# Last chunk of the FFN's second product: T1 and T2 unsplit in DRAM, loads in order of use, last pair's sums on GpSimd, T3 multiplied behind B22

## The chip, the cores and the metric

The kernel runs on one core of one Trainium2 chip. The metric is the device time of one execution in microseconds (us), lower is better. A core has TensorE (PE in the profile; its weight loads are PEld), VectorE (DVE), ScalarE (ACT) and GpSimd (POOL), each with a queue of its own that is worked off in order, and SyncE (SP), whose queue issues this kernel's DMA transfers, also in order.

## The reference

Two layers on a sequence of 1024 positions with 1024 channels. Each layer is a token mixer (FoX attention in layer 0, gated linear attention in layer 1) and then a SwiGLU channel mixer. Only the channel mixer matters here:

```python
def swiglu(h, w_in, w_out):
    gate, up = jnp.split(h @ w_in, 2, axis=-1)
    return (jax.nn.silu(gate) * up) @ w_out
...
        h = modulate(rms_norm(x, norm2_g[i]), sh2, sc2)
        x = x + g2[:, None, :] * swiglu(h, ffn_w_in[i], ffn_w_out[i])
    return rms_norm(x, final_g)
```

The hidden width is 2816, that is 22 tiles of 128 channels. `h @ w_in` is called the first product below, `(...) @ w_out` the second product.

## The kernel before, in words

Channels lie on the 128 partitions, positions along the free dimension, in two halves of 512. Every fp32 operand is split into a rounded high part (`hi`, made by an ACT copy) and the remainder (`lo`, a subtraction, mostly on DVE); a block product is then three matmuls, hi by hi, hi by lo and lo by hi (`mm3`, L304 to L307). Both products are computed by a Strassen-like scheme on 2 by 2 blocks with seven block products instead of eight. Its right-hand operands have the names B11, T1, T2, T3, B21, T4, B22: the B are quarters of the hidden activations, the T are sums and differences of them. A block product over four pairs of hidden tiles is 4 x 3 = 12 matmuls of 128x128 by 128x512.

The first product leaves the hidden activations in DRAM (`hid_out`, L1582). B11, B21, B22, T1 and T2 are written already split, as 512 KB tiles of hi and lo; T3 and T4 (`RAWT`) are written unsplit, 256 KB each, and are split when they come back.

The second product runs over the 11 pairs of hidden tiles in three chunks of 3, 4 and 4 pairs (`ODS`). Chunks 0 and 1 loop over four pairs of output tiles (i = 0 to 3), with seven block products each, in PSUM tiles that the profile names `p`; their results are added up by DVE in SBUF (L1860). In the last of these passes the five sums per output pair that undo the scheme (L1874 to L1878), and the four gate-and-residual steps (L1880), follow each pair; the sums are on GpSimd for i = 0 to 2 and on VectorE for i = 3. The residual is loaded by `load_xr` into four small buffers, the cycle `late_raw`, which unsplit T3 and T4 also use.

The last chunk (L1909 to L1940) multiplies for each group g = 0 to 3 of output tiles B11, T1, T2, B22 and T3, in PSUM tiles `f0a`, `f0b` (layer 0) and `f1a`, `f1b` (layer 1); `pa` takes B11, T2 and T3 one after another, and DVE adds its state to the output (`out_add`, L1899) between them. Then B21 and T4 follow over all output tiles (`f0e`, `f1e`), with the sums of squares for the next norm.

`part(c_)` (L1759) is a generator that loads the 28 tiles of a chunk, one per step, and splits the unsplit ones; `advance(n)` drives it to step n at written places between the products. For the last chunk the order is B11, T1, T2, B22, T3, B21, T4, four tiles each. Unsplit tiles are loaded up to three steps ahead. A tile can only be loaded when the block product of the chunk before that read its slot is done.

Weights are loaded raw (`op_raw`, L920, tiles `xv`), four of them per group, combined by three or four GpSimd operations (L938, L939, L940 and L950 or L956) and split (L174 on ACT, L175 on DVE; tiles `o`). They run about five block products ahead, as far as their six slots reach.

The program's text gives priorities. The order on each engine is fixed before the run by a scheduler that works from its own estimate of the times, so a product can stand on the engine earlier or later than in the text, unless a dependency forbids it. `tc.issue_after(x)` adds such a dependency on order alone.

Of the kernel before, what the change touches and what calls it, by code (L numbers as in the profile page):

```python
# [9 lines left out]
F32 = mybir.dt.float32  # L10
# [6 lines left out]
P = 128  # L17
S = 1024
# [35 lines left out]
def trunk(ctx, tc, x, c, ada_w, ada_b, norm1_g, norm2_g, ffn_w_in, ffn_w_out,  # L54
          fox_w_in, fox_b_f, fox_w_out, gla_w_in, gla_w_a2, gla_b_a, gla_g_o,
          gla_w_out, final_g, out, dbg=None, stop=None):
    nc = tc.nc
# [281 lines left out]
    xr = Ring(big, take(8))  # L339
# [62 lines left out]
    for t in range(6):  # L402
        nt, src = (4, rows2[0:8, :]) if t < 4 else (2, crow)
# [20 lines left out]
    def mcol(l, j, k):  # L424
        return modc[:, l, j, k:k + 1]
# [10 lines left out]
    def last_of(e):  # L436
        return next(i for i in reversed(nc.cur_bb.bb.instructions) if i.engine == ENG[e])
# [753 lines left out]
    for n, (d, hf) in enumerate(rest0):  # L1191
# [25 lines left out]
        if n in late_tr:  # L1217
            tp, i = late_tr[n]
# [258 lines left out]
    early = [s_ for s_ in rest if s_ in list(vring.q) + qk_all + list(cumr.q)]  # L1477
# [14 lines left out]
    def ffn(l, oh, xs, slots, nm, mid, norm_end, each=None, blocks=None):  # L1492
# [19 lines left out]
        hi = lambda t: t[:, 0]  # L1512
        lo = lambda t: t[:, 1]
# [59 lines left out]
        hid_d = {}  # L1573
        for i in range(NPR):
            for nm_ in ("B11", "B12", "B21", "B22", "T1", "T2", "T3", "T4"):
                if nm_ == "B12":
                    continue
                raw_ = nm_ in RAWT
                hid_d[(nm_, i)] = tc.dram_tile([P, HALF] if raw_ else [P, 2, HALF], F32,
                                               name=f"hid{l}_{nm_}{i}")  # L1580

        def hid_out(nm_, i, y):  # L1582

            if nm_ not in RAWT:
# [75 lines left out]
        B11, B21 = b["B11"], b["B21"]  # L1660
# [43 lines left out]
        B12, B22, T1, T2 = b["B12"], b["B22"], b["T1"], b["T2"]  # L1704
# [26 lines left out]
        T3 = b["T3"]  # L1731
# [4 lines left out]
        T4 = b["T4"]  # L1736
# [22 lines left out]
        def part(c_):  # L1759

            raw_ = late_raw if c_ else early_raw
            n_k = ODS[c_]
            nms = ONAMES if c_ < OC - 1 else ENAMES
            order = list(range(7 * n_k)) if c_ else list(FIRST)
            tiles, ys = o[c_], {}
            for nm_ in ONAMES:
                tiles[nm_] = [None] * n_k
            at = lambda n: (nms[n // n_k], n % n_k)

            def load_raw(n):  # L1770
                nm_, k = at(n)
                if nm_ in RAWT and n not in ys:
                    ys[n] = raw_()
                    nc.sync.dma_start(ys[n], hid_d[(nm_, OAT[c_] + k)])

            for j, n in enumerate(order):
                nm_, k = at(n)
                t = tiles[nm_][k] = big.tile([P, 2, HALF], FR, tag=SL[c_][n], name=f"{nm_}o{l}{c_}{k}")
                load_raw(n)
                if nm_ in RAWT:  # L1780
                    split_t(t, ys[n])
                else:
                    nc.sync.dma_start(t.bitcast(F32), hid_d[(nm_, OAT[c_] + k)])
                for ahead in order[j + 1:j + 4]:
                    load_raw(ahead)
                yield

        xr, zs = {}, {}

        def load_xr(i, views):  # L1790
            for a in range(2):
# [42 lines left out]
        for c_ in range(OC - 1):  # L1834
            last = c_ == OC - 2
            spare = (9, 2)[c_]
            n_nxt[0] = 0
            nxt[0] = part(c_ + 1)
            for i in range(4):
                Y1, Y3 = (xs[2 * i][:, hsl(hf)] for hf in range(2))  # L1840
                Y2, Y4 = (xs[2 * i + 1][:, hsl(hf)] for hf in range(2))
                Z1, Z5 = zs[i][:, 0], zs[i][:, 1]

                def p_(j):
                    ps = prod(feed.next(), o[c_][ONAMES[j]])
                    if i < 3:
                        advance(spare * (7 * i + j + 1) // 21)
                    else:
                        advance(UPTO[c_][j])
                    if last and j == (2 if i < 3 else 4):  # L1850
                        if i == 3:
                            sv.extend(Views(sb[0:2], 2, [HALF], f"se{l}").v)
                        load_xr(i, late_raw if i < 3 else Cycle(sv))
                    return ps

                def onto(y, ps, first=True):
                    if c_ == 0 and first:
                        nc.scalar.copy(y, ps)
                    else:
                        nc.vector.tensor_add(y, y, ps)  # L1860
# [12 lines left out]
                V = nc.vector if i == 3 else nc.gpsimd  # L1873
                V.tensor_add(Y1, Y1, Z1)  # L1874
                V.tensor_add(Y4, Y4, Z1)
                V.tensor_sub(Y2, Y4, Y2)
                V.tensor_add(Y4, Y4, Z5)
                V.tensor_sub(Y3, Y4, Y3)  # L1878
                for (a, hf), v_ in (((0, 0), Y1), ((1, 0), Y2), ((1, 1), Y4), ((0, 1), Y3)):
# [9 lines left out]
        def chained(ps, nm_, start, behind=(), cs=slice(0, HALF)):  # L1889
            w, t = feed.next(), oe[nm_]  # L1890
            for k in range(4):
                with ExitStack() as es:
                    for ins in behind if k == 0 else ():
                        es.enter_context(tc.issue_after(ins))
                    mm3(ps, w.hi[:, k, :], w.lo[:, k, :], hi(t[k])[:, cs], lo(t[k])[:, cs],
                        start and k == 0, k == 3, True)

        def out_add(m, hf, ps):
            nc.vector.scalar_tensor_tensor(xs[m][:, hsl(hf)], ps, mcol(l, 5, m), xs[m][:, hsl(hf)],  # L1899
                                           op0=ALU.mult, op1=ALU.add)  # L1900
# [5 lines left out]

        tmp = None if each else Views(slots["to"], 2, [HALF], f"te{l}")
        sq = SumFew(sv, 0)
        for g in range(4):  # L1909
            if g == 3:  # L1910
                feed.depth = 3
            pa, pb = (pj([P, HALF], F32, f"f{l}{nm_}{g}") for nm_ in "ab")
            chained(pa, "B11", True)
            advance(20 + (8 * (5 * g + 1)) // 15)
            out_add(2 * g, 1, pa)
            chained(pb, "T1", True)
            advance(20 + (8 * (5 * g + 2)) // 15)
            out_add(2 * g + 1, 0, pb)
            chained(pa, "T2", False)
            advance(20 + (8 * (5 * g + 3)) // 15)  # L1920
            out_add(2 * g, 0, pa)
            chained(pb, "B22", False)
            advance(20 + (8 * (5 * g + 4)) // 15)
# [55 lines left out]
    order = ex_sl + slots["hid"] + slots["b"][4:] + slots["to"] + x_slots + slots["b"][:4]  # L1979
# [540 lines left out]
```

## Time and profile before

| | us |
|---|---|
| runs of the kernel, three | 2356.21, 2358.49, 2358.67 |
| their median | 2358.49 |
| the profiled execution's own time | 2358.25 |
| its span, first to last instruction | 2356.5 |
| DVE, ACT and POOL busy in the span | 1778.1, 1122.5, 1126.3 |

A row of the timeline gives the start, the duration, the engine, the line, the operation with output and inputs, and in brackets the idle time of the engine in front of it and what ended it. A row of the windows view gives, for a stretch of the span, each engine's busy time (with the number of its instructions), the TensorE clock that was granted (1.00 is full), the busy share of the DMA engines and the rate. DMA rows under `SPq` give the issue, not the transfer. Matmuls overlap, so the pace is read from start to start.

### The profile page before, as it was taken

How to read it: one execution, taken by the hardware profiler on the slowest of the kernel's cores; microseconds unless marked ns; L12 is line 12 of the kernel's file. 1: busy time of each engine (PE TensorE's matmuls, PEld its weight loads, DVE VectorE, ACT ScalarE, POOL GpSimd, SP SyncE). 2: the span in 40 equal slices, each digit the busy share in tenths (PEclk: the TensorE clock that was granted, in tenths of full speed). 3: DMA queues.
4: the chain of work that ended last, by engine and by line, in shares of the span. 5: the costliest groups of instructions: out<-in, count | busy, mean ns of one | idle time of the engine just before them, and what ended most of it. 6: DMA issues, size and time to landing. Idle time of an engine off the chain costs nothing. (4 is left out here: it accounts for less than half of the span.)

```text
span 2356.5 us, 35548 instructions
## 1 busy us (share of the span) xinstructions
PE 2327.9 (99%) x12168; PEld 1980.9 (84%) x12168; DVE 1778.1 (75%) x2957; ACT 1122.5 (48%) x2166; POOL 1126.3 (48%) x995
## 2 busy tenths in 40 slices
PE   8999999999999999999999999999999999999999
PEld 7888888888888888888878898898888888888878
DVE  6578787886788888886787665678787777876776
ACT  6656655665443333345234644344453333345235
POOL 1334544533445666664643431345446665665631
PEclk8999999999999999999999999999999999999999
DMA  8423333332435545458674442554435444458574
GB/s 266 144 90 106 102 121 95 121 129 96 143 101 167 187 161 173 160 192 298 224 272 158 138 134 87 146 182 166 145 111 164 165 150 155 148 204 298 199 277 136
DMA packets 349614, 383.38 MB, mean 163 GB/s; under 512 B 25372, under 2 KB 286648, under 8 KB 349432
## 3 DMA queue, kind: packets, MB, share of 16 engines
q1 hardware_dynamic: 349432, 381.11, 49.1%
q8 instruction: 96, 1.57, 0.3%
q14 instruction: 86, 0.70, 0.1%
HBM read 279.76 MB, written 101.25 MB: 162 GB/s over the span
## 5 line engine op out<-in xcount | busy, mean ns | idle before, releaser
L174 ACT CAST o_s<-xv_s 128x512 fp32r<-128x512 f32 (+1 forms) x392 | 236.5, 610 | 343.0 <-PE p_b L307 250.0
L175 DVE TENSOR_TENSOR o_s<-xv_s,o_s 128x512 fp32r<-128x512 f32 (+1 forms) x392 | 331.9, 851 | 44.8 <-ACT o_s L174 44.0
L307 PE MATMUL p_b<-B,o_s 128*128 128x512 f32 x608 | 236.0, 389 | 0.0
L306 PE MATMUL p_b<-B,o_s 128*128 128x512 f32 x608 | 235.9, 389 | 0.0
L305 PE MATMUL p_b<-B,o_s 128*128 128x512 f32 x608 | 235.4, 390 | 0.0
L938 POOL TENSOR_TENSOR ex_s<-xv_s,xv_s 128x512 f32<-128x512 f32 (+1 forms) x64 | 96.2, 1503 | 259.0 <-DMA xv_s<-in_ffn_w_in_dram 119.9
L1291 POOL TENSOR_SCALAR lp_s<-lp_s,st 128x128 f32<-128x128 f32 (+7 forms) x128 | 98.0, 769 | 246.3 <-DVE st L1290 231.1
L305 PE MATMUL p_b<-T,o_s 128*128 128x512 f32 x480 | 186.8, 389 | 0.0
L306 PE MATMUL p_b<-T,o_s 128*128 128x512 f32 x480 | 186.7, 389 | 0.0
L307 PE MATMUL p_b<-T,o_s 128*128 128x512 f32 x480 | 181.1, 389 | 0.0
L307 PEld LDWEIGHTS p_b<-B,o_s 128*128 128x128 f32 x608 | 114.1, 188 | 23.8
L305 PEld LDWEIGHTS p_b<-B,o_s 128*128 128x128 f32 x608 | 114.2, 188 | 23.7 <-DVE x L1657 0.2
L306 PEld LDWEIGHTS p_b<-B,o_s 128*128 128x128 f32 x608 | 114.2, 188 | 23.5
L1289 ACT ACTIVATE lp_s<-lp_s,st 128x128 f32<-128x128 f32 (+7 forms) x128 | 99.3, 776 | 58.0 <-DVE st L1285 56.7
L940 POOL TENSOR_TENSOR xv_s<-ex_s,xv_s 128x512 f32<-128x512 f32 (+1 forms) x64 | 94.4, 1475 | 59.5 <-DVE o_s L175 56.5
L1657 DVE TENSOR_TENSOR ex_s<-ex_s,p_b 128x512 f32<-128x512 f32 x140 | 94.3, 682 | 37.4 <-PE p_b L307 37.3
L174 ACT CAST pt_s<-t_b 128x512 fp32r<-128x512 f32 (+1 forms) x160 | 79.7, 547 | 72.9 <-PE t_b L1311 72.3
L950 POOL TENSOR_TENSOR xv_s<-xv_s,xv_s 128x512 f32<-128x512 f32 x48 | 65.2, 1358 | 96.3 <-issue 52.3
L175 DVE TENSOR_TENSOR pt_s<-t_b,pt_s 128x512 fp32r<-128x512 f32 (+1 forms) x160 | 96.3, 630 | 15.9 <-ACT pt_s L174 15.4
L246 POOL TENSOR_TENSOR w_l_s<-w__s,w_h_s 128x256 fp32r<-128x256 f32 x90 | 69.4, 799 | 76.6 <-ACT w_h_s L242 58.8
L307 PEld LDWEIGHTS p_b<-T,o_s 128*128 128x128 f32 x480 | 90.1, 188 | 18.7
L306 PEld LDWEIGHTS p_b<-T,o_s 128*128 128x128 f32 x480 | 90.1, 188 | 18.6
(1532 smaller groups left out, 7396.8 us busy)
## 6 DMA issues: line engine op xcount, KB each, us to landing
xv_s<-in_ffn_w_in_dram SPq DMA_DIRECT2D x176, 256.0 KB, 3.2
hid_B<-x SPq DMA_DIRECT2D x66, 512.0 KB, 2.8
ad_s<-in_ada_w_dram SPq DMA_DIRECT2D x384, 64.0 KB, 2.3
hid_T<-x SPq DMA_DIRECT2D x44, 512.0 KB, 2.9
xv_s<-in_ffn_w_out_dram SPq DMA_DIRECT2D x88, 256.0 KB, 3.2
ada_s<-in_ada_w_dram SPq DMA_DIRECT2D x96, 128.0 KB, 2.8
T2o<-hid_T SPq DMA_DIRECT2D x22, 512.0 KB, 7.6
T1o<-hid_T SPq DMA_DIRECT2D x22, 512.0 KB, 8.6
```

The source lines that it names most:

```text
L174: nc.scalar.copy(hi, src)
L175: nc.vector.tensor_sub(lo, src, hi.bitcast(F32))
L246: (nc.gpsimd if i < 3 else nc.vector).tensor_sub(lo[:, cs], rw[:, cs], hi[:, cs].bitcast(F32))
L305: nc.tensor.matmul(ps, ah, bh, start=start, stop=False, skip_group_check=chain)
L306: nc.tensor.matmul(ps, ah, bl, start=False, stop=False, skip_group_check=chain)
L307: nc.tensor.matmul(ps, al, bh, start=False, stop=stop, skip_group_check=chain)
L938: nc.gpsimd.tensor_add(s1, a21, a22)
L940: nc.gpsimd.tensor_sub(a11, s1, a11)
L950: nc.gpsimd.tensor_sub(r[A12], r[A12], r[A11])
L1289: nc.scalar.activation(lp, lp, AF.Exp, bias=mcur, scale=-1.0, accum_out=st[:, qi, 2:3])
L1291: nc.gpsimd.tensor_scalar(lp, lp, st[:, qi, 3:4], 1.0, op0=ALU.mult, op1=ALU.mult)
L1657: nc.vector.tensor_add(d, d if src is None else dest(G, src), ps)
```

## The change

For the last chunk's four pairs (i from 7 to 10) T1 and T2 are also written unsplit. When they come back, ACT makes hi and GpSimd makes lo. The last chunk's loads are chained on SP in the order in which `part` issues them, with two steps of look-ahead instead of three. The five sums of the last output pair go from VectorE to GpSimd, and its four gate steps are put off and issued one by one between the first products of the last chunk. T3's four splits move from the end of the pass before into the first group of the last chunk. Each T3 product may not be issued ahead of what stands before it on TensorE, the group's B22 among it; and no product of B21 or T4 may be issued ahead of the last group.

```diff
-    RAWT = ("T3", "T4")
+    def is_raw(nm_, i):
+        return nm_ in ("T3", "T4") or nm_ in ("T1", "T2") and i >= OAT[-1]
...
+            def fetch(dst, src):
+                with tc.issue_after(pre[0]) if pre else ExitStack():
+                    nc.sync.dma_start(dst, src)
+                if c_ == OC - 1:
+                    pre[:] = [last_of("S")]
...
+                if nm_ in ("T1", "T2") and n in ys:
+                    nc.scalar.copy(hi(t), ys[n])
+                    nc.gpsimd.tensor_sub(lo(t), ys[n], hi(t).bitcast(F32))
+                elif n in ys:
                     split_t(t, ys[n])
                 else:
-                    nc.sync.dma_start(t.bitcast(F32), hid_d[(nm_, OAT[c_] + k)])
-                for ahead in order[j + 1:j + 4]:
+                    fetch(t.bitcast(F32), hid_d[(nm_, OAT[c_] + k)])
+                for ahead in order[j + 1:j + (3 if c_ == OC - 1 else 4)]:
                     load_raw(ahead)
...
-                V = nc.vector if i == 3 else nc.gpsimd
+                V = nc.gpsimd
...
+                if i == 3:
+                    ends.extend(gates_)
+                else:
+                    for f in gates_:
+                        f()
-            advance(20 if last else 28)
+            advance(16 if last else 28)
...
+        def meanwhile(g, n):
+
+            if g == 0:
+                advance((18, 20, 20, 20, 21)[n])
+            else:
+                advance(21 + (7 * (5 * g - 4 + n)) // 15)
+            if ends:
+                ends.popleft()()
...
-            chained(pa, "T3", False)
-            advance(min(28, 20 + (8 * (5 * g + 5)) // 15))
+            chained(pa, "T3", False, [last_of("P")])
+            meanwhile(g, 4)
...
+        early = last_of("P")
         behind = norm_end(0, sq, tmp)
...
-                chained(ps, "T4" if m % 2 else "B21", True, [ins for m_, ins in behind or () if m >= m_], cs)
+                chained(ps, "T4" if m % 2 else "B21", True,
+                        [early] + [ins for m_, ins in behind or () if m >= m_], cs)
```

More of the change, by code (lines that the diff above doesn't have):

```diff
@@ L1577, in ffn @@
                     continue
-                raw_ = nm_ in RAWT
+                raw_ = is_raw(nm_, i)
                 hid_d[(nm_, i)] = tc.dram_tile([P, HALF] if raw_ else [P, 2, HALF], F32,
@@ L1582, in hid_out @@
         def hid_out(nm_, i, y):
-            if nm_ not in RAWT:
+            if not is_raw(nm_, i):
                 t = hb()
@@ L1768, in part @@
             at = lambda n: (nms[n // n_k], n % n_k)
+            def fetch(dst, src):
[3 more added lines that the diff above has]
+                    pre[:] = [last_of("S")]
             def load_raw(n):
                 nm_, k = at(n)
-                if nm_ in RAWT and n not in ys:
+                if is_raw(nm_, OAT[c_] + k) and n not in ys:
                     ys[n] = raw_()
-                    nc.sync.dma_start(ys[n], hid_d[(nm_, OAT[c_] + k)])
+                    fetch(ys[n], hid_d[(nm_, OAT[c_] + k)])
+            pre = []
             for j, n in enumerate(order):
@@ L1779, in part @@
                 load_raw(n)
-                if nm_ in RAWT:
+                if nm_ in ("T1", "T2") and n in ys:
+                    nc.scalar.copy(hi(t), ys[n])
+                    nc.gpsimd.tensor_sub(lo(t), ys[n], hi(t).bitcast(F32))
+                elif n in ys:
                     split_t(t, ys[n])
                 else:
-                    nc.sync.dma_start(t.bitcast(F32), hid_d[(nm_, OAT[c_] + k)])
-                for ahead in order[j + 1:j + 4]:
+                    fetch(t.bitcast(F32), hid_d[(nm_, OAT[c_] + k)])
+                for ahead in order[j + 1:j + (3 if c_ == OC - 1 else 4)]:
                     load_raw(ahead)
                 yield
-        xr, zs = {}, {}
+        xr, zs, ends = {}, {}, deque()
         def load_xr(i, views):
@@ L1878, in ffn, with gated @@
                 V.tensor_sub(Y3, Y4, Y3)
-                for (a, hf), v_ in (((0, 0), Y1), ((1, 0), Y2), ((1, 1), Y4), ((0, 1), Y3)):
+                def gated(a, hf, v_, i=i):
                     nc.vector.scalar_tensor_tensor(v_, v_, mcol(l, 5, 2 * i + a), xr[(a, hf)],
                                                    op0=ALU.mult, op1=ALU.add)
-            advance(20 if last else 28)
+                gates_ = [lambda a=a, hf=hf, v_=v_: gated(a, hf, v_)
+                          for (a, hf), v_ in (((0, 0), Y1), ((1, 0), Y2), ((1, 1), Y4), ((0, 1), Y3))]
+                if i == 3:
[4 more added lines that the diff above has]
+            advance(16 if last else 28)
         ada1.flush()
@@ L1913, in ffn @@
             chained(pa, "B11", True)
-            advance(20 + (8 * (5 * g + 1)) // 15)
+            meanwhile(g, 0)
             out_add(2 * g, 1, pa)
             chained(pb, "T1", True)
-            advance(20 + (8 * (5 * g + 2)) // 15)
+            meanwhile(g, 1)
             out_add(2 * g + 1, 0, pb)
             chained(pa, "T2", False)
-            advance(20 + (8 * (5 * g + 3)) // 15)
+            meanwhile(g, 2)
             out_add(2 * g, 0, pa)
             chained(pb, "B22", False)
-            advance(20 + (8 * (5 * g + 4)) // 15)
+            meanwhile(g, 3)
             out_add(2 * g, 0, pb)
             done_(sq, 2 * g, 2 * g, 0)
-            chained(pa, "T3", False)
-            advance(min(28, 20 + (8 * (5 * g + 5)) // 15))
+            chained(pa, "T3", False, [last_of("P")])
+            meanwhile(g, 4)
             out_add(2 * g + 1, 0, pa)
```

## The prediction

> **What bounds the kernel now.** The head of the page comes first.
>
> ```profile
> span 2356.5 us, 35548 instructions
> PE 2327.9 (99%) x12168; PEld 1980.9 (84%) x12168; DVE 1778.1 (75%) x2957; ACT 1122.5 (48%) x2166; POOL 1126.3 (48%) x995
> ```
>
> TensorE is the bound: 28.6 us of the span are left in which it does nothing. The change removes no matmul, so it can only gain where TensorE stands still or runs slow. The waits of TensorE, from the waits view, say where in the changed stage that is.
>
> ```profile
> PE f1a_b L307 <- DVE o_s L175: 2.1, 1, 2.1
> PE f0a_b L307 <- DVE o_s L175: 1.2, 1, 1.2
> PE f0a_b L305 <- DVE x L1899: 0.8, 1, 0.8
> PE f1a_b L305 <- DVE x L1899: 0.8, 1, 0.8
> PE sp_b L776 <- DVE se_s L818: 0.3, 1, 0.3
> ```
>
> All are in the last chunk (f0 is layer 0, f1 layer 1): 5.2 us in five waits. The timeline of TensorE in layer 1 shows what they cost from start to start, and that more is lost behind the first.
>
> ```profile
> 2263.41 0.39 PE L306 MATMUL f1b_b<-T1o,o140s_s 128*128 128x512 f32 x1
> 2263.64 0.39 PE L307 MATMUL f1b_b<-T1o,o140s_s 128*128 128x512 f32 x1
> 2264.22 0.40 PE L306 MATMUL f1a_b<-B11o,o_s 128*128 128x512 f32 x1
> 2266.71 0.50 PE L307 MATMUL f1a_b<-B11o,o_s 128*128 128x512 f32 x1 [2.10 <-DVE o_s L175]
> 2268.20 0.58 PE L307 MATMUL f1a_b<-B11o,o_s 128*128 128x512 f32 x1
> 2271.57 0.44 PE L306 MATMUL f1a_b<-T2o,o_s 128*128 128x512 f32 x1
> 2273.24 0.40 PE L307 MATMUL f1a_b<-T2o,o_s 128*128 128x512 f32 x1
> 2274.48 0.51 PE L305 MATMUL f1a_b<-T3o,o_s 128*128 128x512 f32 x1 [0.84 <-DVE x L1899]
> ```
>
> Undisturbed matmuls start 0.23 apart (first two rows), a block product of twelve takes 2.72. The first wait costs 2266.71 - 2264.22 - 0.23 = 2.26. The fifth and sixth row have seven matmuls between them, so eight steps in 3.37 us where 1.82 would do: 1.55 lost. The T3 wait costs 2274.48 - 2273.24 - 0.23 = 1.01. Layer 1 loses 4.8. Layer 0, whose 1.2 and 0.8 grow by the same 0.16 each, loses 1.4 + 1.0 = 2.4. Together **7.2 us**.
>
> The windows view tells why those eight steps are slow, and what the DMA engines do.
>
> ```profile
> 1194.00:1224.00 30.00, 27.81 (x121) 22.02 (x120) 23.42 (x35) 7.47 (x13) 8.56 (x6) 1.00 1.04 390
> 2250.00:2280.00 30.00, 27.06 (x110) 21.38 (x110) 21.55 (x32) 7.63 (x13) 7.96 (x6) 0.94 1.04 389
> 2268.00:2271.00 3.00, 3.00 (x9) 2.39 (x8) 3.00 (x5) 0.00 (x0) 0.00 (x0) 0.54 1.05 381
> 2280.00:2292.00 12.00, 12.00 (x54) 9.94 (x54) 10.46 (x15) 6.60 (x13) 6.15 (x5) 1.00 0.39 117
> ```
>
> In the third row the granted clock is 0.54: the 2.1 us wait is followed by a stretch at about half speed. (The Trainium skill, "TensorE: Matmul & The Clock Gate", section "Why this matters for your kernels", sets the gap that brings the half clock at over about 3 us; here 2.1 were enough. By the page the 1.55 would not be part of the wait's price; I go by the row.) The first two rows show 30 us in each layer in which the DMA engines are full (1.04, 390 GB/s); in the fourth it is over.
>
> Now the cause of the first wait, from the timelines of ACT, DVE and SP.
>
> ```profile
> 2251.24 0.32 SPq L1774 DMA_DIRECT2D ex_s<-hid_T  x1
> 2261.64 1.66 ACT L1535 CAST T3o<-ex_s 128x512 fp32r<-128x512 f32 x3 [4.44 <-DMA ex_s<-hid_T]
> 2263.21 0.62 ACT L174 CAST o_s<-xv_s 128x512 fp32r<-128x512 f32 x1
> 2262.30 0.69 DVE L1536 TENSOR_TENSOR T3o<-ex_s,T3o 128x512 fp32r<-128x512 f32 x1 [3.02 <-ACT T3o L1535]
> 2265.97 0.69 DVE L175 TENSOR_TENSOR o_s<-xv_s,o_s 128x512 fp32r<-128x512 f32 x1
> ```
>
> T3's last load was issued at 2251.24, into the full DMA queue. ACT stood 4.44 us in front of T3's copy, DVE 3.02 in front of its subtraction, and the weight of the next group's B11, queued behind T3 on both, got its low half at 2266.66. That is what TensorE waited for, and T3 itself was not needed before 2274.
>
> **The change part by part.** *T1 and T2 unsplit.* Eight tiles of 256 KB come in place of 512 KB. At 390 GB/s, 256 KB take 0.67 us: 5.4 us less of the full stretch per layer. At the end of the first product eight splits on ACT and DVE go; TensorE has no wait there, so this is worth nothing. What is added is eight ACT copies and eight GpSimd subtractions, between the products of the last pair.
>
> *Order of the loads.* On SP today B21, which is used last, stands in front of a weight load:
>
> ```profile
> 2262.91 1.69 SPq L1783 DMA_DIRECT2D B21o<-hid_B  x3
> 2264.95 0.38 SPq L920 DMA_DIRECT2D xv_s<-in_ffn_w_out_dram  x1
> 2273.91 1.27 POOL L938 TENSOR_TENSOR ex_s<-xv_s,xv_s 128x512 f32<-128x512 f32 x1 [19.98 <-DMA xv_s<-in_ffn_w_out_dram]
> 2275.87 1.23 DVE L175 TENSOR_TENSOR o141s_s<-ex_s,o141s_s 128x512 fp32r<-128x512 f32 x1 [1.45 <-ACT o141s_s L174]
> ```
>
> The weight load took nine us, and the T1 weight of group 1 that hangs on it was ready at 2277.10. Four B21 tiles of 512 KB behind it are another 5.4 us. Both together about empty the queue, so B22, T3 and the weights should land within 3 to 5 us. The chain has a price too: a load that waits for its buffer holds every load behind it on SP, weights included.
>
> *T3 in the first group, behind B22.* T3's copies no longer stand ahead of the next B11's weight with nothing to do, and the text asks for that weight two products later. This takes the two first waits and the slow stretch. And twelve matmuls, 2.72 us, come between T2's end and T3 on the same PSUM tile; `out_add` needs the 1.01 measured above, so both T3 waits go, with 1.7 to spare.
>
> *B21 and T4 behind the last group.* The matmuls are the same. Three whole products, 8.2 us, now stand between the last T3 and the sums of squares in layer 0: the 0.3 of the fifth wait goes. The cover lost: a late weight of the last group can no longer be bridged by them; in the quoted waits no such weight is late, so nothing.
>
> *Sums and gates.* Five DVE operations go to GpSimd. Their prices, and GpSimd's room:
>
> ```profile
> 2256.20 0.68 DVE L1874 TENSOR_TENSOR x<-x,z 128x512 f32<-128x512 f32 x1
> 2234.30 1.74 POOL L1875 TENSOR_TENSOR x<-x,z 128x512 f32<-128x512 f32 x1
> 2243.53 1.61 POOL L1878 TENSOR_TENSOR x<-x,x 128x512 f32<-128x512 f32 x1 [1.29 <-DVE x L1860]
> 2249.23 1.62 POOL L939 TENSOR_TENSOR xv_s<-xv_s 128x512 f32<-128x512 f32 x1
> 2252.64 1.29 POOL L950 TENSOR_TENSOR xv_s<-xv_s,xv_s 128x512 f32<-128x512 f32 x1
> 2250.22 1.18 DVE L175 TENSOR_TENSOR o140s_s<-ex_s,o140s_s 128x512 fp32r<-128x512 f32 x1
> 2238.00:2274.00 36.00, 33.54 (x139) 26.71 (x137) 27.51 (x40) 7.17 (x12) 10.41 (x8) 0.95 0.92 336
> ```
>
> DVE saves 5 x 0.68 = 3.4 us. GpSimd gets five sums of 1.29 to 1.74 (6.5 to 8.7) and eight subtractions of 1.29 to 1.62 (10.3 to 13.0). From 2245.14, where the third pair's last sum ends, to 2273.91, where group 1's weights claim it, GpSimd has 28.8 us; the weights of group 0 take four operations there, 5.2 to 6.5. The need is 22.0 to 28.2: it fits, barely. Of DVE: an L175 beside a GpSimd operation takes 1.18 (2250.22, inside 2249.23 to 2250.85), alone 0.68 like any such operation here. Thirteen more GpSimd operations at 0.5 each cost DVE 6.5, less the 3.4: 3.1 more, against 36 - 27.5 = 8.5 idle in the last row. Hidden.
>
> The gates wait on DVE for GpSimd's sums; behind them stand `out_add` and weight splits. Their outputs, tiles 6 and 7, are used only in group 3. By the bound from below a gate waits for nothing; from above it holds DVE for one sum, 1.74, which the 2.72 of a product cover. I take nothing.
>
> **The sum.** 7.2 + 0.3 = 7.5 us can go. I leave 0.5 for first-use waits of the size of the fifth. The profiled execution's own time, span 2356.5 and 1.75 around it, is 2358.25, 0.24 below the median of the runs. 2358.25 - 7.0 = **2351.3 us**. If all goes, 2350.8; where waits up to 3 us stay, 2353.8.
>
> **The rivals.** *The wait moves to group 1's T1.* In the text's order that product starts six products after the pass, at 2258.42 + 16.3 = 2274.7 in layer 1. Its weight was ready 3.2 us after its load released GpSimd. If the load comes no earlier, because SP is held by T1's and T2's buffers, TensorE waits 2277.1 - 2274.7 = 2.4 in each layer: 2358.25 - 7.2 + 4.8 = **2355.9**, less where it is half. For it: the chain on SP; GpSimd takes the load's place as what is late when it has its 28 us of work. Against it: 10.8 us fewer in the queue.
>
> The start that this and the next rival count from:
>
> ```profile
> 2258.42 0.39 PE L305 MATMUL f1a_b<-B11o,o_s 128*128 128x512 f32 x1
> ```
>
> *GpSimd is late with T2, and the kernel is slower.* If the last pair's sums are placed ahead of T2's subtractions, the eighth of these ends only after all the work, 2245.1 + 22.0 to 28.2 = 2267.1 to 2273.3, in the middle 2270.2. T2's fourth part is due in the text's order at 2258.42 + 2 x 2.72 + 9 x 0.227 = 2265.9: a wait of 4.3, and as it is longer than 2.1, the slow stretch of 1.55 behind it. 2358.25 - 7.2 + 2 x 5.85 = **2362.8**. It is slower than before if T2 is ready after about 2268.0 (2.05 + 1.55 per layer eat the 3.6 gained). Against it: in the text the sums stand behind T2's splits, and sums behind make T2 ready at 2245.1 + 15.5 to 19.5 = 2260.6 to 2264.6.
>
> *VectorE is locked out.* If each of the 13 operations held DVE for its whole 1.29 to 1.74, DVE would need 16.8 to 21.7 more, less 3.4 and 8.5 idle: 4.9 to 9.8 too much per layer, 2358.25 - 7.2 + 2 x 7.3 = **2365.7**. Against it: the row above waits only until the GpSimd operation beside it ends, half of it. (The Trainium skill, "SBUF — State Buffer", section "Who interferes with whom", says that a DVE operation with two SBUF inputs and a GpSimd operation that reads SBUF exclude each other fully, the later blocked until the first ends; the trace agrees, 1.18 against 0.68, and by that rule this loss is its upper end.)
>
> *It doesn't do what it says.* The scheduler places weights or sums anew and as much is lost elsewhere in the stage: **2358**.
>
> **How the numbers follow.** About 0.2% (4.7 us) is what can be told from no change. Chances: forecast 0.52, wait at T1 0.24, GpSimd late 0.12, lock-out 0.04, no effect 0.08. Faster by over 0.2% is below 2353.8: nearly all of the forecast and a little of the second, 0.53. Slower is above 2363.2 by that bound: half of GpSimd late, most of the lock-out, with a like share for what both could do together: 0.11. The rest, 0.36, is within. The range is 2348 to 2361: below the 2350.8 by 2.8 for waits elsewhere that a new schedule may take, above up to the smaller half of GpSimd late. The forecast's own range is 2349 to 2354.
>
> **What would show it.** Right: the five quoted waits are gone, the clock is 1.00 through the last chunk of layer 1, DMA is full for some 20 us instead of 30, B22 stands in front of T3, and group 1's first weight operation on GpSimd starts before 2271. Wrong: a TensorE wait of over 1 us on T2 (GpSimd) or on group 1's T1 (weights), or SP standing in front of an L1774-like load while weights queue behind it.

## The result and the profile after

The changed kernel takes 2369.73 us (median of 6 runs, 2366.94 to 2372.53) against 2359.19 for the kernel before (6 runs, 2356.21 to 2360.67): ratio 1.0046, 95% interval 1.0033 to 1.0059. It is slower by 10.5 us. The forecast was 2351.3, and the range ended at 2361.

The head of the page of the changed kernel:

```profile
span 2365.2 us, 35547 instructions
PE 2331.9 (99%) x12168; PEld 1985.0 (84%) x12168; DVE 1767.9 (75%) x2931; ACT 1122.2 (47%) x2166; POOL 1170.9 (50%) x1021
```

GpSimd does 44.6 us more, 26 operations, which are the 13 per layer that the change gives it. VectorE is busy 10.2 us less over the whole run. The waits of TensorE in the last chunk (f0 is layer 0, f1 layer 1; total, times, longest):

```profile
PE f0a_b L305 <- DVE x L1920: 4.2, 2, 3.3
PE f1a_b L305 <- DVE x L1920: 3.4, 1, 3.4
PE f1b_b L305 <- DVE x L1920: 1.4, 1, 1.4
PE f0b_b L305 <- DVE x L1920: 1.4, 1, 1.4
PE f1a_b L307 <- DVE o_s L175: 0.8, 2, 0.6
PE f0a_b L307 <- DVE o_s L175: 0.7, 1, 0.7
```

Of the five waits quoted before, the 2.1 and the 1.2 for the low half of group 1's B11 weight shrank to 0.6 and 0.7, and the 0.3 is gone. The two of 0.8 for `out_add` (L1920 now) in front of T3 grew to 3.3 and 3.4, and 1.4 in front of the first B22 of each layer is new; all waits for `out_add` together are 10.4 us. So TensorE still waits for VectorE, now at other places. The windows view, over the same part of layer 1 as in the prediction (30 us from 8.5 us before the last chunk's first matmul):

```profile
2256.50:2286.50 30.00, 25.86 (x111) 20.11 (x109) 23.74 (x23) 10.77 (x20) 29.23 (x19) 1.00 0.96 328
```

The DMA engines moved 328 GB/s where they moved 389, that is 1.8 MB less in the 30 us; eight tiles of 256 KB less are 2.1 MB. Their busy share went from 1.04 to 0.96, so the full stretch did not shrink to the 20 us that the prediction named. The fifth engine of the row is GpSimd: 29.23 of 30 us. The longest wait, from the timelines of TensorE, VectorE and GpSimd:

```profile
2287.74 0.50 PE L305 MATMUL f1a_b<-T3o,o_s 128*128 128x512 f32 x1 [3.38 <-DVE x L1920]
```

```profile
2276.14 1.77 DVE L1893 SCALAR_TENSOR_TENSOR x<-x,modc,se_s 128x512 f32<-128x512 f32 x1 [1.18 <-POOL x L1888]
2277.83 0.74 DVE L1920 SCALAR_TENSOR_TENSOR x<-f1b_b,modc,x 128x512 f32<-128x512 f32 x1
2278.49 1.10 DVE L1538 TENSOR_TENSOR T3o<-ex_s,T3o 128x512 fp32r<-128x512 f32 x1
2279.52 1.78 DVE L175 TENSOR_TENSOR o141s_s<-ex_s,o141s_s 128x512 fp32r<-128x512 f32 x1
2281.22 3.47 DVE L1538 TENSOR_TENSOR T3o<-ex_s,T3o 128x512 fp32r<-128x512 f32 x2
2284.62 2.41 DVE L1893 SCALAR_TENSOR_TENSOR x<-x,modc,se_s 128x512 f32<-128x512 f32 x2
2286.95 1.40 DVE L1920 SCALAR_TENSOR_TENSOR x<-f1a_b,modc,x 128x512 f32<-128x512 f32 x2
```

```profile
2274.37 1.74 POOL L1888 TENSOR_TENSOR x<-x 128x512 f32<-128x512 f32 x1
2279.00 1.75 POOL L941 TENSOR_TENSOR xv_s<-xv_s 128x512 f32<-128x512 f32 x1
2280.71 1.74 POOL L1890 TENSOR_TENSOR x<-x,x 128x512 f32<-128x512 f32 x1
2282.41 1.74 POOL L942 TENSOR_TENSOR xv_s<-ex_s,xv_s 128x512 f32<-128x512 f32 x1
```

T2's matmuls ended at 2277.0, but the `out_add` that frees the tile for T3, the first of the two at 2286.95, ended only at about 2287.7. In front of it on VectorE stand T3's splits, a weight's low half and two gates, without a gap. Those from 2279.52 to 2284.69 take as long as the GpSimd operations beside them: the subtraction at 2279.52 takes 1.78 where one alone takes 0.68. The first two rows are the wait of 1.4 in front of B22: a put-off gate stands 1.18 us on VectorE until GpSimd has made its sum (2274.37 to 2276.11), then takes 1.77, and the `out_add` that frees the tile for B22 stands behind it. The groups of the windows 2253 to 2286 (after) and 2246.4 to 2279.4 (before), the same stretch, give the means. After:

```profile
L1538 DVE TENSOR_TENSOR T3o<-ex_s,T3o 128x512 fp32r<-128x512 f32 x4 | 5.7, 1442 | 0.0
L1893 DVE SCALAR_TENSOR_TENSOR x<-x,modc,se_s 128x512 f32<-128x512 f32 x3 | 5.3, 1763 | 1.2 <-POOL x L1888 1.2
L1872 DVE TENSOR_TENSOR x<-x,p_b 128x512 f32<-128x512 f32 x6 | 3.9, 676 | 0.0
```

Before:

```profile
L1536 DVE TENSOR_TENSOR T3o<-ex_s,T3o 128x512 fp32r<-128x512 f32 x4 | 2.7, 685 | 3.0 <-ACT T3o L1535 3.0
L1880 DVE SCALAR_TENSOR_TENSOR x<-x,modc,se_s 128x512 f32<-128x512 f32 x4 | 2.9, 746 | 0.0
L1860 DVE TENSOR_TENSOR x<-x,p_b 128x512 f32<-128x512 f32 x6 | 4.0, 675 | 0.0
```

T3's splits went from 685 to 1442 ns, the gates from 746 to 1763. The third row did not move: it takes one input from PSUM (`p_b`), and is not held up.

### The profile page after: what moved, and what is told of

Its sections match the earlier page's. It is cut to its first block, busy times and chain, and to the rows that moved or that the text cites. A ratio compares the mean times of both kernels' runs of the same rounds, so it can differ in the third digit from the quotient of the medians.

```text
span 2365.2 us, 35547 instructions
## 1 busy us (share of the span) xinstructions
PE 2331.9 (99%) x12168; PEld 1985.0 (84%) x12168; DVE 1767.9 (75%) x2931; ACT 1122.2 (47%) x2166; POOL 1170.9 (50%) x1021
## 5 line engine op out<-in xcount | busy, mean ns | idle before, releaser
L175 DVE TENSOR_TENSOR o_s<-xv_s,o_s 128x512 fp32r<-128x512 f32 (+1 forms) x392 | 337.6, 865 | 64.9 <-ACT o_s L174 64.2
L940 POOL TENSOR_TENSOR ex_s<-xv_s,xv_s 128x512 f32<-128x512 f32 (+1 forms) x64 | 97.5, 1523 | 216.8 <-DMA xv_s<-in_ffn_w_in_dram 113.6
L175 DVE TENSOR_TENSOR pt_s<-t_b,pt_s 128x512 fp32r<-128x512 f32 (+1 forms) x160 | 96.3, 630 | 15.9 <-ACT pt_s L174 15.4
```

What stands on the lines that cost most here:

```text
L175: nc.vector.tensor_sub(lo, src, hi.bitcast(F32))
L940: nc.gpsimd.tensor_add(s1, a21, a22)
```

## The experiments

The theory after this view is that GpSimd locks VectorE out (called the lock or the exclusion below): VectorE is the engine that is late; the subtractions of T1 and T2, brought from the end of the first product into this stretch, and the five sums hold it up from GpSimd. The rivals: the put-off gates are the cost; the loads, or T3's place, are; VectorE is simply full, whoever does the new work.

One profiled execution is no measure of some us. In the stretch from 60 to 66 us, whose code is the same in both, the granted clock was 1.00 in the profile of before and 0.56 in that of after. So the table gives beside the times the length of the changed stage itself in each profile: from the start of the first to the last matmul on f0 (and f1), plus one step, from the timeline. Ratios are against the kernel before on the same chip, over all runs of the comparison, and so not exactly the quotients of the medians. The stage lengths have a limit too: behind most of the waits comes a stretch in which matmuls start 0.43 apart instead of 0.23, at about half the clock. Counted by these steps it makes 0 and 1.4 us (layer 0 and 1) before, 1.8 and 0.2 after, 3.0 in either layer with the idle subtractions on GpSimd, 1.6 with them on VectorE, 1.4 with both jobs on VectorE, and nothing in the three fastest kernels, whose stages agree within 0.1 us.

| kernel | us, median | ratio, 95% interval | f0 stage | f1 stage |
|---|---|---|---|---|
| before | 2359.2 to 2360.7 | | 82.4 | 89.4 |
| after | 2369.73 | 1.0046 (1.0033 to 1.0059) | 87.4 | 91.5 |
| sums back on VectorE | 2371.35 | 1.0039 (1.0024 to 1.0054) | 87.8 | 92.9 |
| T1, T2 subtractions on VectorE | 2368.98 | 1.0035 (1.0025 to 1.0045) | 86.9 | 91.5 |
| both on VectorE | 2362.23 | 1.0004 (0.9992 to 1.0016) | 84.6 | 89.2 |
| gates later | 2371.23 | 1.0038 (1.0023 to 1.0053) | 87.4 | 92.4 |
| T1, T2 split as before | 2355.05 | 0.9979 (0.9968 to 0.9990) | 79.9 | 84.1 |
| the same, sums on VectorE ("S") | 2353.92 | 0.9973 (0.9960 to 0.9985) | 79.9 | 84.1 |
| S, gates at once | 2354.85 | 0.9978 (0.9969 to 0.9988) | 79.9 | 84.2 |
| S, loads not in order | 2364.78 | 1.0029 (1.0017 to 1.0041) | 84.7 | 90.3 |
| S, 8 idle subtractions on GpSimd | 2373.74 | 1.0065 (1.0050 to 1.0080) | 89.4 | 94.9 |
| S, 8 idle subtractions on VectorE | 2365.48 | 1.0015 (1.0002 to 1.0028) | 85.5 | 90.4 |
| before, T3 behind B22 | 2369.34 | 1.0029 (1.0018 to 1.0040) | 86.2 | 92.0 |
| before, sums on GpSimd | 2361.90 | 1.0007 (0.9998 to 1.0017) | 83.3 | 87.2 |
| before, T1, T2 unsplit, 3 ahead | 2364.26 | 1.0023 (1.0013 to 1.0033) | 86.0 | 91.7 |
| before, T1, T2 unsplit, 2 ahead | 2369.21 | 1.0045 (1.0030 to 1.0060) | 84.7 | 89.9 |

**Undoing one part of the change at a time.** First the sums back on VectorE:

```diff
-                V = nc.gpsimd
+                V = nc.vector if i == 3 else nc.gpsimd
```

> The changed kernel with the last pair's five sums back on VectorE; the put-off gates and all else stay. Beside before (2359.2) the changed kernel takes 2369.7. Theory 'exclusion' (13 more GpSimd operations fill GpSimd and stretch VectorE's two-input operations beside it, so VectorE is late with out_add and T3): GpSimd has a gap again, T3's splits fall from 1.44 us to about 1.0, the waits of 3.4 on T3 to under 2; time about 2362. Rival 'queue order' (the gates stand ahead of out_add on VectorE and wait there for GpSimd's sums): the gates no longer wait for another engine, the T3 wait goes to about 0; time 2359 or less. Rival 'loads' (T3 comes late because its buffers hang on T2 and the loads are chained): T3's copies still stand about 3 us on DMA and time stays at 2367 or more.

Then T1's and T2's subtractions on VectorE:

```diff
-                    nc.gpsimd.tensor_sub(lo(t), ys[n], hi(t).bitcast(F32))
+                    nc.vector.tensor_sub(lo(t), ys[n], hi(t).bitcast(F32))
```

> The changed kernel with T1's and T2's low halves made by VectorE; the sums stay on GpSimd. 'Exclusion': eight fewer operations on GpSimd, five remain; T3's splits at about 1.0 us, T3 wait under 2, time about 2361. 'Queue order': the gates still wait for GpSimd's sums ahead of out_add; the sums come earlier, but some 1 to 2 us of the T3 wait stay, time 2364. 'Loads': T2's buffers come free earlier, T3's copies wait under 1 us, time 2360.

The longest waits of the one and of the other:

```profile
PE f1a_b L307 <- DVE o_s L175: 5.3, 1, 5.3
PE f0a_b L307 <- DVE o_s L175: 4.9, 1, 4.9
```

```profile
PE f0a_b L307 <- DVE o_s L175: 4.1, 1, 4.1
PE f1a_b L307 <- DVE o_s L175: 4.1, 1, 4.1
```

In both, the wait for T3 is gone, and about the same amount stands in front of the low half of group 1's B11 weight, which the scheduler multiplies ahead of group 0's T2. Moving one of the two jobs to VectorE moves the wait, not the time. No theory had both times right. The loads' fits the first in its number (2367 or more) and in its sign, T3's copies standing up to 4.1 us on DMA; but TensorE does not wait for T3 there, and VectorE works without a gap from 2263.59 to the low half at 2277.57 that it does wait for. For the second that theory had 2360. Then the gates, popped only in group 1. This one also changes what is computed: the residual of the last pair is partly overwritten before the late gates read it.

```diff
-            if ends:
+            if ends and g == 1:
                 ends.popleft()()
```

> The changed kernel with the four put-off gates issued in group 1 and not in group 0; GpSimd's work is the same. 'Exclusion': GpSimd stays full for some 33 us, T3's splits stay at 1.4 us, and the T3 wait shrinks by the gates' own share only, 2.4 of the ten us that out_add is late: about 2367. 'Queue order': out_add of T2 no longer stands behind a gate that waits for the last sum; the T3 wait falls from 3.4 to under 1 in both layers, time 2361 to 2363. 'Loads': no change, 2369.

2371.23, with waits of 2.7 for T3's `out_add` left in both layers: the gates' place is not the cause of the lost time.

**T3's place by itself**, in the kernel before:

```diff
-            chained(pa, "T3", False)
+            chained(pa, "T3", False, [last_of("P")])
```

> The kernel before with one line: T3 may not be issued ahead of its group's B22. By the prediction's step the two T3 waits of 0.8 go (2.0 from start to start): about 2357 against 2359.2. Against it: B22 is loaded after B21 in this kernel and lands at about 2279 in layer 1, so T3, now behind all of B22, can't start before; the weights behind it move too, and the time stays the same or rises by 1 to 3 us.

```profile
PE f1b_b L305 <- DMA B22o<-hid_B: 3.2, 1, 3.2
PE f0b_b L305 <- DMA B22o<-hid_B: 3.2, 1, 3.2
```

T3's wait is gone, but B22, which is now needed first, is still in the DMA queue. This part costs time without the order of the loads, more than the 1 to 3 us that were thought possible.

**The change without the unsplit T1 and T2**, which tells most:

```diff
     def is_raw(nm_, i):
-        return nm_ in ("T3", "T4") or nm_ in ("T1", "T2") and i >= OAT[-1]
+        return nm_ in ("T3", "T4")
```

> The changed kernel with T1 and T2 of the last chunk split before they go to DRAM, as in the kernel before; load order, T3's place, the gates and the sums on GpSimd stay as changed. Theory (the 16 splits of T1 and T2 per layer, brought into the stretch where VectorE and GpSimd serve the last pair's sums and gates, make these two late whichever of them does it): ScalarE loses 8 copies and GpSimd 8 subtractions per group of loads, the sums on GpSimd run from about 7 us earlier, the wait for T3's out_add (4.2 and 3.4) is gone or below 1.5, stage lengths come back to 82 to 85 us and the time to 2358 to 2364. Rival (the sums and gates put off are the cost by themselves): the wait for T3's out_add stays near 3 and the time near 2369. Rival (bytes matter): 2 MB more per layer are moved, B22 and T3 land late, waits for DMA appear before T3 or B22.

And the same with the sums on VectorE, called S from here on:

> As the run with T1 and T2 split before DRAM, and the last pair's five sums on VectorE as in the kernel before: what is left of the change is the order of the transfers, T3 behind B22 and split between the products, and the gates put off by a product each. Theory (VectorE and GpSimd hold each other up in this stretch): with nothing on GpSimd VectorE's two-input operations are at their short durations, the five sums take 3.5 to 4.5 us on VectorE, no wait before the low half of group 1's B11 above 1.5 us, and the time is 2352 to 2358, faster than the kernel before by about the waits that the transfers cost there (up to 6 us). Rival (the load order and T3's place bring nothing, since another wait ends last at the same place): 2358 to 2362. Rival (put-off gates hold VectorE): a wait of 2 us or more before an out_add of group 0 remains.

2355.05 and 2353.92: both are faster than the kernel before, by 0.21% and 0.27%, and than the 2358 to 2364 that the first's theory had, and both stages are about 2.5 and 5.2 us shorter. The only wait of S in the last chunk:

```profile
PE f0b_b L305 <- ACT o_s L174: 1.1, 1, 1.1
```

So the unsplit T1 and T2 cost the changed kernel 15 us, and without them it does most of what the forecast wanted. The rival that the 2 MB more per layer would be felt falls: no wait for a DMA is left. Where the sums run makes 1.1 us, inside the intervals.

**The parts by themselves in the kernel before.** T1 and T2 unsplit alone (the lines of `is_raw`, of `hid_out` and the ACT and GpSimd split of the change), and the sums alone (`V = nc.gpsimd`):

> The kernel before with one part of the change alone: T1 and T2 of the last chunk unsplit in DRAM, their high half copied by ScalarE and their low half subtracted on GpSimd behind the load. Sums on VectorE, order of loads and T3 as before. Theory (these splits are the cost): the time goes up by 5 to 12 us, to 2364 to 2372; VectorE's sums beside the subtractions take over 1 us each instead of 0.75, and waits for T2 or for the low half of group 1's B11 appear. Rival (the sums and gates are the cost): 2355 to 2360.

> The kernel before with one word changed: the five sums of the last pair on GpSimd, the gates straight behind them on VectorE as there. Theory (GpSimd has little else there without the T1 and T2 subtractions): the five sums take 1.3 to 1.8 us each, some 8 us in all, the gates wait for them on VectorE and hold out_add of group 0; 2360 to 2366. Rival (the sums are the whole cost of the change): 2367 or more. Rival (they cost nothing): within 0.2% of the kernel before.

The first of them changes what is computed: with loads three steps ahead, a T1 tile lands in a buffer whose residual is still to be read. The same with two steps ahead, which computes all:

> The kernel before with T1 and T2 of the last chunk unsplit in DRAM (low half subtracted on GpSimd) and raw loads two tiles ahead in the last chunk as in the changed kernel, so that no raw load is ordered between a residual's load and its gate. Theory (the 16 subtractions and copies of T1 and T2 are the cost by themselves, through VectorE held up): 2362 to 2368, the low half of group 1's B11 late by 4 us as in the run with three tiles ahead. Rival (there the early raw load was the cost, not the splits): 2356 to 2360, no such wait.

2364.26 and 2369.21 with it, 2361.90 with the sums alone. The unsplit T1 and T2 alone are enough for a slower kernel; the sums alone make no difference that can be told. In the profile of the kernel with two steps, the stage explains only 2.8 of the 9.3 us; the part ahead of the first stage had 4.0 more than in the profile of before and the part between the stages 3.8 more, nearly all of it in code that is the same. Whether its median lies so high for that reason stays open.

**The lock by itself.** S with one subtraction on GpSimd for each T1 and T2 tile loaded, into a dead buffer (extra work, the output is as it was):

```diff
                     fetch(t.bitcast(F32), hid_d[(nm_, OAT[c_] + k)])
+                    if c_ == OC - 1 and nm_ in ("T1", "T2"):
+                        nc.gpsimd.tensor_sub(zs[0][:, 0], hi(t).bitcast(F32), lo(t).bitcast(F32))
```

> The kernel with T1 and T2 split before DRAM and sums on VectorE, and in it one subtraction on GpSimd for each T1 and T2 tile of the last chunk that is loaded (8 per layer): same size and engine as in the changed kernel, its result written to a dead buffer that nobody reads. Nobody waits for these, so what they cost, they cost through VectorE alone. Theory (GpSimd's two-input operations hold up VectorE's): VectorE's two-input operations beside them take 1.0 to 1.8 us instead of 0.7 to 0.9; the low half of group 1's B11 or an out_add comes late; 2356 to 2366 against 2354 without them, and the more of it, the larger the share of the lock in the 17 us that the changed kernel with sums on VectorE lay behind this one. Rival (the cost was that products wait for T1's and T2's own splitting, and for the buffers that it holds): 2353 to 2355, no difference.

2373.74, 20 us above S and above the 2356 to 2366 expected, though nobody waits for these results. VectorE and GpSimd in the timelines of layer 1:

```profile
2271.03 1.77 DVE L1888 TENSOR_TENSOR x<-x,z 128x512 f32<-128x512 f32 x1
2272.72 0.67 DVE L1874 TENSOR_TENSOR x<-x,p_b 128x512 f32<-128x512 f32 x1
2273.32 1.18 DVE L175 TENSOR_TENSOR o_s<-xv_s,o_s 128x512 fp32r<-128x512 f32 x1
2274.42 1.77 DVE L1890 TENSOR_TENSOR x<-x 128x512 f32<-128x512 f32 x1
2276.12 1.75 DVE L1895 SCALAR_TENSOR_TENSOR x<-x,modc,se_s 128x512 f32<-128x512 f32 x1
2277.80 1.75 DVE L1891 TENSOR_TENSOR x<-x,z 128x512 f32<-128x512 f32 x1
```

```profile
2272.33 6.67 POOL L1797 TENSOR_TENSOR z<-T2o 128x512 f32<-128x512 f32 x4
2278.96 1.71 POOL L940 TENSOR_TENSOR ex_s<-xv_s,xv_s 128x512 f32<-128x512 f32 x1
```

Four idle subtractions in a row take 1.67 each, and VectorE's sums beside them go at the same pace: 1.75 to 1.77 each, where S has all five at 0.68. Only the row with a PSUM input keeps its 0.67. The longest wait of TensorE is again for the low half of group 1's B11, 4.7 in either layer:

```profile
PE f1a_b L307 <- DVE o_s L175: 4.7, 1, 4.7
```

Another way to such a wait would be GpSimd's queue: the weights' sums stand behind the idle subtractions there. It is not what happened here. ACT had made this weight's high half by 2271.30, and VectorE works without a gap from 2266.57 to its low half, which ends at 2281.21. From the first of the five sums to this low half VectorE has the same eleven operations in the same order in both kernels: they take 7.3 us in S (2256.04 to 2263.38) and 13.6 here (2267.62 to 2281.21), though none was added to VectorE.

**Lock, or no room?** The same idle subtractions on VectorE itself (`nc.vector` in the added line), and the changed kernel with its subtractions and sums all on VectorE (the first two diffs together):

> The kernel with T1 and T2 split before DRAM and sums on VectorE, with the eight idle subtractions per layer on VectorE instead of GpSimd; nobody reads their results. They take 8 times 0.7 = 5.5 us of VectorE per layer. Theory (exclusion: an operation on GpSimd costs VectorE 1.1 us or more, one on VectorE 0.7): 2356 to 2366, clearly below the 2373.7 of the same subtractions on GpSimd. Rival (VectorE is simply full): 2370 or more, as there.

> The changed kernel with T1's and T2's subtractions and the five sums all on VectorE, so that GpSimd has only the weights' sums. 16 operations of some 0.7 us more per layer on VectorE than in the kernel with T1 and T2 split before DRAM, and no exclusion. Theory (the exclusion of the two engines is most of the loss): 2356 to 2364, better than the changed kernel with the sums alone or the subtractions alone on VectorE (2371, 2369). Rival (VectorE has no room there at all): 2366 to 2372, no better than those, with group 1's B11 low half 4 us late.

2365.48 and 2362.23. (The second has 8 more subtractions per layer on VectorE than S, not the 16 that its expectation says.) The waits of the first and its window from the last chunk's start on:

```profile
PE f1a_b L305 <- DVE x L1922: 2.1, 1, 2.1
PE f0a_b L305 <- DVE x L1922: 2.1, 1, 2.1
PE f1a_b L307 <- DVE o_s L175: 1.8, 1, 1.8
PE f0a_b L307 <- DVE o_s L175: 1.8, 1, 1.8
```

```profile
2266.90:2288.00 21.10, 17.18 (x67) 13.39 (x66) 20.42 (x29) 4.24 (x7) 7.17 (x4) 0.92 1.00 356
```

VectorE (the third engine) is busy 20.42 of 21.1 us; in S it is 15.79 over the same length, but what is idle there comes behind group 1's B11, too late to help. Eight subtractions of 0.68 are 5.4 us, and the stages grew by 5.6 and 6.2 over S, 1.6 of it at half clock behind the waits. On GpSimd the same eight made the stages 9.5 and 10.8 longer, 3.0 of it at half clock. So both halves of the question are answered yes: added work is not hidden on VectorE here, and the same operation is dearer on GpSimd than on VectorE, by 3.9 and 4.6 us for eight, or 2.5 and 3.2 without the half clock. The two are not cleanly divided: with the work on VectorE, its later operations meet the weights' sums on GpSimd, and the lock is back for three of them:

```profile
2274.58 1.78 DVE L1797 TENSOR_TENSOR z<-T2o 128x512 f32<-128x512 f32 x1
2274.18 1.62 POOL L941 TENSOR_TENSOR xv_s<-xv_s 128x512 f32<-128x512 f32 x1
```

**The order of the loads**, taken out of S:

```diff
-                if c_ == OC - 1:
-                    pre[:] = [last_of("S")]
```

> The kernel with T1 and T2 split before DRAM and sums on VectorE, without the ties that keep the last chunk's loads in the order of use (the scheduler's own order instead). Theory (the load order is what lets T3 stand behind B22 without waiting; T3 behind B22 alone brought waits of 3 us for B22): a wait of 2 to 3.5 us for B22's load in one or both layers, 2357 to 2363. Rival (the order of loads brings nothing, T3's place does): 2352 to 2356, no wait for a DMA in group 0.

```profile
PE f1b_b L305 <- DMA B22o<-hid_B: 3.5, 1, 3.5
PE f0b_b L305 <- DMA B22o<-hid_B: 3.5, 1, 3.5
```

The issues on SP in this kernel show why: all four tiles of B21, used last, stand ahead of B22.

```profile
2266.35 2.96 SPq L1774 DMA_DIRECT2D B21o<-hid_B  x4
2270.94 1.04 SPq L1774 DMA_DIRECT2D B22o<-hid_B  x2
2273.80 1.59 SPq L1774 DMA_DIRECT2D B22o<-hid_B  x2
```

2364.78, 10.9 above S: the tie is what makes T3's place pay. Last, the gates straight behind the sums in S (the `ends` queue left out):

> The kernel with T1 and T2 split before DRAM and sums on VectorE, with the last pair's four gates straight behind the sums instead of one behind each product. Theory (order of transfers and T3's place are the gain; gates are cheap where VectorE isn't held up): 2353 to 2357, at most 1 us of waiting for out_add of group 0's B11. Rival (putting the gates off is a gain by itself): 2356 to 2360, a wait of 2 to 3 us for the first out_add or for group 1's B11.

2354.85 against 2353.92: putting the gates off is neither gain nor loss that can be told.

## Why the prediction was wrong, by its own steps

**The 7.5 us of waits to be had: right.** S has them: its stages are 2.5 and 5.2 us shorter than before, 7.7 in all (the prediction had 2.4 and 4.8), only one wait of 1.1 us is left, and its median is 6.1 us lower. The steps for T3 behind B22 and for the order of the loads held too, though only both together: T3's place without the order of the loads costs, in the kernel before and in S. The order without T3's place was not run.

**T1 and T2 unsplit: the step that failed.** The prediction said that the splits at the end of the first product cost nothing there, which is right, and listed what is added between the products of the last pair without asking whether VectorE could bear it there. It put its cost into the next step, "Hidden".

**"Thirteen more GpSimd operations at 0.5 each cost DVE 6.5 ... against 36 - 27.5 = 8.5 idle in the last row. Hidden.": wrong twice.** The price was measured on one operation that met a GpSimd operation half-way (the L175 at 2250.22 runs past that operation's end at 2250.85, not inside it); where the two engines follow each other without a gap, a two-input operation of VectorE takes 0.76 (T3's splits), 1.0 (gates) or 1.1 us longer (sums beside the idle subtractions). This price stood in the profile of before: 59 of its 128x512 subtractions at L175 and L1536 take 1.74 to 1.82, all beside a GpSimd operation, as this one beside L940 on GpSimd (2176.62, 1.61 long):

```profile
2177.00 1.78 DVE L175 TENSOR_TENSOR o130s_s<-ex_s,o130s_s 128x512 fp32r<-128x512 f32 x1
```

And the cover was not there. The 8.5 us were idle time over 36 us: 3.0 in front of T3's late loads, 2.5 behind group 1's B11 and T2, 2.4 in front of gates that wait for GpSimd's sums. Between the pass's last products and group 1's B11 VectorE has a row of work with a due time. The run with the idle subtractions on VectorE shows it: 5.4 us of work made 5.6 and 6.2 us of stage, the half clock behind the waits included.

**"The gates ... I take nothing": wrong in place of price.** The gate at 2276.14 waits 1.18 us for GpSimd's sum, as the prediction allowed, but then takes 1.77 beside GpSimd's next operations, and TensorE stands 1.4 us in front of B22: the product did not cover it. At 2284.62 two more gates stand on VectorE ahead of T2's `out_add`; GpSimd's last sum had ended at 2282.45, so what held these was VectorE's own work. But it is not their being put off that costs: where VectorE is not held up, gates at once and gates put off are the same.

**"B22, T3 and the weights should land within 3 to 5 us": wrong, and not what brought the gain.** From issue to landing, in the median of each kind, the loads of this stretch of layer 1 took 6.5 to 7.0 us in the changed kernel but for B22's 3.6, and 7.6 to 8.2 in S, whose DMA engines stay full (1.05, 386 GB/s, 2250 to 2280 us). The rows of the DMA view for the unsplit tiles, first the changed kernel (one of T2, four of T3 and one of T4, issued from 2263 to 2277.5), then S (T3 and T4, 2258 to 2276), end with the median:

```profile
ex_s<-hid_T SPq DMA_DIRECT2D x6, 256.0 KB, 6.5
ex_s<-hid_T SPq DMA_DIRECT2D x6, 256.0 KB, 7.7
```

S gains because the loads that are needed first are issued first. In the changed kernel each T3 load also needs a buffer that a subtraction of T2 on GpSimd frees: the four were issued at 2265.27, 2269.34, 2272.74 and 2274.44, each just behind the end of such a subtraction (the second behind 2267.58 + 1.74 = 2269.32). So T3's splits came late too.

**The rival "VectorE is locked out", given 0.04, is what happened in the main**, at another price. It said 7.3 us per layer; between the changed kernel and S lie 7.5 and 7.4 us of stage, and that the numbers agree is luck. The rival let each of 13 operations hold VectorE for its whole 1.29 to 1.74 and took off 8.5 of idle time; in the runs an operation costs 1.1 at most, and the idle time is no cover. With the subtractions and sums all on VectorE, 4.7 and 5.1 of stage are lost already; doing them on GpSimd adds 2.8 and 2.3. The times divide the loss otherwise (ratios 0.9973, 1.0004 and 1.0046, so 7.3 and 9.9 us), and the stages hold unlike amounts of half clock, so the shares of lock and missing room stay open; that both count is shown by the idle subtractions. "GpSimd is late with T2" did not come about: T2's last subtraction ended at 2274.4, but the scheduler had put group 1's B11 ahead of T2, and no wait for GpSimd shows. "The wait moves to group 1's T1" did not either. The rule of the Trainium skill that was cited beside the rival ("SBUF — State Buffer", "Who interferes with whom") is borne out as to which operations exclude each other. As a price, the whole GpSimd operation is too much: where both engines are busy, sums of 0.68 take 1.75 to 1.77, that is 1.1 longer, beside operations that take 1.28 alone and 1.67 here.

Of the 10.5 us the stages account for 5.0 + 2.1 = 7.1. The two profiled executions differ by 1.6 more outside the stages, where the stretch with the half clock at 60 to 66 us makes about 2.0 and other places give some back; the other 1.8 is that the profiled executions lie 2.8 (after) and 0.9 us (before) below their medians. Single profiles don't split it further.

## What to carry to other kernels

Before work is moved to GpSimd, look at which stretch it lands in and whether VectorE has two-input operations due there; there, in these runs, an operation on GpSimd cost VectorE more (1.1 us) than doing it itself (0.7), and a mean of idle time over a longer stretch was no cover. Read the price where the two engines follow each other without a gap, not from one pair. A step that costs nothing where it stands (a split at a place where nobody waits) is to be left there. Reordering products pays only when the loads are put in the same order, so try such parts together and alone: here two of the change's parts make 0.27% and a third had buried them.

## What the runs showed of the hardware that was not expected

A VectorE operation with one input in PSUM is not held up by GpSimd: 676 ns after, 675 before, in the same stretch in which those with two SBUF inputs went from 685 to 1442. The half clock behind a stall is not a matter of the stall's length alone: in the changed kernel the same wait for T3 was 3.3 us in layer 0 and 3.4 in layer 1, and behind it the granted clock differs:

```profile
1227.50:1231.00 3.50, 3.45 (x9) 2.76 (x10) 3.50 (x6) 1.55 (x3) 0.00 (x0) 0.59 0.23 68
2287.70:2291.00 3.30, 3.26 (x14) 2.71 (x15) 3.30 (x6) 1.36 (x3) 0.00 (x0) 1.00 0.23 66
```

In the kernel before, 2.1 us were followed by 0.54; with the sums alone on GpSimd, 2.4 us in layer 0 were followed by 1.00 (1215 to 1220 us). What decides it was not tried.
